# First-norm squares added on VectorE before one sum on TensorE, and a wider column of ones in the own-key sum

## The chip, the core and the metric

The kernel runs on one core of a Trainium2 chip. The metric is the device time of one execution in microseconds (us). The engines are TensorE (PE; its weight loads are listed apart as PEld), VectorE (DVE), ScalarE (ACT), GpSimd (POOL) and SyncE (SP, which issues the DMA transfers). They run their own queues in order and wait for each other by semaphores.

## The reference

One layer of a streaming encoder: 512 frames, 1024 channels, float32. What touches the change:

```python
def rmsnorm(x, g):
    y = x32 * lax.rsqrt(jnp.mean(x32 * x32, axis=-1, keepdims=True) + EPS)
    return (y * g).astype(x.dtype)
...
h = rmsnorm(x, norm_mix_g[l])
z = h @ w_in[l]      # all projections of three branches
...
# branch B, in chunks: decayed attention of each frame over the keys up to itself, and a carried state
attn = jnp.einsum("bhtk,bhsk,bhtsk->bhts", qx, kx, decay)
```

The three branches are a softmax attention with forget gates (6 heads), a gated linear recurrence (4 heads of 128 keys, 96 values) and a convolution module (256 channels, 31 taps). They are projected, merged by sigmoid gates, projected again and added to x; a second RMS norm and a gated feed-forward block of width 2816 follow.

## The kernel before

**Layout.** x lies transposed: eight tiles x0 to x7 of 128 channels by 512 frames. Each float32 product is made of three TensorE matmuls: both operands are split into a high part (suffix h; wh for weights), a rounded copy made by ScalarE, and a low part (l; wl), the remainder made by VectorE. A weight unit (`wunit`, L320) is thus a DMA to wr, a ScalarE cast to wh and a VectorE subtraction to wl; there are three buffers of each.

**The first norm.** The products start from x times the norm's gain; the factor of each frame, 1/rms, is multiplied in later, when a product leaves PSUM. The factor needs the sum of the squares of 1024 channels, which lie on partitions of eight tiles. ScalarE squares each tile into n1sq0 to n1sq7. `norm_rstd` (L425) then multiplies every 128 frames of every square tile (as the weights) with 32 columns of 1/1024 and adds all eight tiles up in PSUM: 4 x 8 matmuls into n1ms. Twelve small VectorE instructions (nv, nrt, nry, nra) take the inverse root: `rt1`, one factor for each frame, frames on partitions. `spread` (L411) transposes it on TensorE (n1rT), copies the row (n1row) and sends it through DRAM to all partitions: `rb1`, the tile n1rB. The second norm (L965) works the same way, but hands over one tile, which GpSimd has added up, so that it has 4 matmuls (n2ms).

**Who needs the factors.** The first product, him (values of branch B), has frames on partitions: four PSUM banks, evacuated by ScalarE with `rt1` to hv. The products behind it, cb, ca, cb, ca, hf, hq, f0m and so on, have frames along the free axis and are evacuated by VectorE with n1rB. Products may hold five of the eight PSUM banks.

**Own-key sum.** In each of the four heads of branch B (`hgrn_head`, L546) the product of the first frame of each 128 with its own key is summed over the 128 key channels: a matmul with one column of ones as weights gives one row (pa), which ScalarE copies to the attention tile (at).

**Order.** Nothing is issued as the code stands. Every call is recorded (`record`, L101) and a planner (`schedule`, L138) plays the kernel through with its own cost for each instruction (`cost`, L235), and writes the order of every engine's queue from that: an instruction is placed where its inputs are due and its engine is free, the lowest priority number first. Priorities are the order of the code plus a base: FIRST (first loads and splits), WPREP (weight units), STAT (squares, sums and factor of the first norm), EVAC (evacuations), then everything else, such as the him matmuls and the 31-tap convolution (cv). The planner's cost of a TensorE instruction goes by the wider of the output and the weights. So a changed instruction can change the order of the queues everywhere behind it. A line number of the trace is mostly L109, the call that issues; instructions are told apart by their tiles.

Of the kernel before, what the change touches and what calls it, by code (L numbers as in the profile page):

```python
# [15 lines left out]
ALU = mybir.AluOpType  # L16
# [13 lines left out]
NM = S // P  # L30
# [246 lines left out]
def body(ctx: ExitStack, tc, xT, wct, wt3, wt1, wdn, par, cst, rst, msk, out):  # L277
# [8 lines left out]
    nc = Plan(tc.nc, CAPS)  # L286
# [6 lines left out]
    def slot(name, dt=F32, kind=None):  # L293
        return nc.tile(spool, [P, S], dt, "s", nm(name), ("s", kind) if kind else ("s",))

    def tiny(name, n, dt=F32):
        return nc.tile(tpool, [P, 32], dt, "tiny", nm(name), ("tiny",))[:, :n]
# [4 lines left out]
    def bank(name, kind="aux"):  # L302
        return nc.tile(ppool, [P, S], F32, "ps", nm(name), ("ps", kind))
# [5 lines left out]
    def pc(name, i=0, n=1):  # L309
        o, _ = PCOLS[name]  # L310
        return pr[:, o + i:o + i + n]

    def cc(name):
        o, w = CCOLS[name]
        return cs[:, o:o + w]

    ident, ones, big = cc("ident"), cc("ones"), cc("big")
# [51 lines left out]
    def split_scaled(src, g, name):  # L369
        hi = slot(name + "h", F32R)  # L370
        nc.scalar.activation(hi, src, AF.Copy, scale=g)
        lo = slot(name + "l", F32R)
        nc.vector.scalar_tensor_tensor(lo, src, g, hi.bitcast(F32), op0=ALU.mult, op1=ALU.subtract)
        return hi, lo
# [73 lines left out]
    xg, w0, sums = [], [], []  # L448
# [3 lines left out]
    def first_weights():  # L452
        k0, k1 = cuts[len(w0)]
        src = wt3[k0 // 2][:, (k0 % 2) * 384:(k0 % 2) * 384 + (k1 - k0) * 384]
        w0.append(wunit(src, (k1 - k0) * 384, f"hi{len(w0)}", FIRST))

    for kt in range(KT):
        with nc.at(FIRST):
            if kt == 0:
                nc.sync.dma_start(pr, par)  # L460
            nc.sync.dma_start(xs[kt], xT[:, kt, :])
        if kt in (0, 1, 3):
            first_weights()
        with nc.at(FIRST):
            xg.append(split_scaled(xs[kt], pc("g1", kt), f"x{kt}"))
        with nc.at(STAT):
            q = slot(f"n1sq{kt}")
            added = nc.scalar.activation(q, xs[kt], AF.Square)
            sums.append(q)
    first_weights()  # L470
    with nc.at(FIRST):
        nc.sync.dma_start(cs, cst)
# [73 lines left out]
    def hgrn_head(h, xf, xq):  # L546
# [50 lines left out]
        for li, L in enumerate(LEVELS):  # L597
# [16 lines left out]
            else:  # L614
# [3 lines left out]
                                        op=ALU.add)  # L618
# [24 lines left out]
        pr0 = tiny("pr0", NM)  # L643
# [1 line left out]
        nc.vector.tensor_tensor(pr0, pr0,  # L645
                                xq.rearrange("p (c t) -> p c t", t=P)[:, :, 0], op=ALU.mult)
        pa = bank("pa")
        nc.tensor.matmul(pa[:1, :NM], ones[:, :1], pr0, start=True, stop=True)
        nc.scalar.copy(atc[:1, :, 0], pa[:1, :NM])
        pi = bank("pi")  # L650
        last = []
# [228 lines left out]


    hgrn_head(0, *hgrn_gemm(0))
    fox_qk(0)
    hgrn_head(1, *hgrn_gemm(1))
    fox_qk(1)
    fox_v()
    hgrn_head(2, *hgrn_gemm(2))
    hgrn_head(3, *hgrn_gemm(3))
    hgrn_norm()
# [64 lines left out]
    for n in range(KT):  # L954
        ps = gemm_c(47 + n, merged, f"wo{n}")
        with nc.at(EVAC):
            nc.vector.tensor_tensor(x1[n], ps, x1[n], op=ALU.add)
            xg2.append(split_scaled(x1[n], pc("g2", n), f"x2{n}"))
            q = slot(f"n2sq{n}")
# [117 lines left out]
```

## Time and profile before

| | |
|---|---|
| median of 3 runs | 826.54 us (826.02 to 826.95) |
| the profiled execution, its time | 826.6 us |
| its span, first to last instruction | 824.8 us |
| TensorE busy | 818.1 us, 99% |
| VectorE busy | 491.0 us, 60% |
| ScalarE busy | 334.4 us, 41% |
| GpSimd busy | 70.3 us, 9% |
| mean granted TensorE clock | 0.996 |

Busy time is summed over the instructions of an engine; the ends of matmuls, which are pipelined, are modelled, so starts are the better guide to TensorE's pace. The granted clock is a share of full speed.

### The profile page before, as it was taken

What the parts mean: (1) busy time and instruction counts of PE and PEld (TensorE: products, weight loads), DVE (VectorE), ACT (ScalarE), POOL (GpSimd) and SP (SyncE); (2) the same over time, 40 slices, a digit from 0 to 9 for tenths busy, and PEclk for the clock granted to TensorE, in tenths of its full rate; (3) what the DMA queues carried; (4) which work ended last, traced back from release to release, by engine and by line L of the source; (5) the groups of instructions that cost most, each with busy time, mean ns of one, the idle gap of its engine ahead of it and who ended that gap; (6) DMA issues with size and microseconds to landing.
All of it is one profiled execution on the core that took longest, in us unless ns stands there. A gap on an engine that the chain in (4) does not pass through costs nothing.

```text
span 824.8 us, 10354 instructions
## 1 busy us (share of the span) xinstructions
PE 818.1 (99%) x4055; PEld 693.2 (84%) x4055; DVE 491.0 (60%) x794; ACT 334.4 (41%) x545; POOL 70.3 (9%) x56
## 2 busy tenths in 40 slices
PE   8999999999999999999999999999999999999998
PEld 7989899878988888888888888888888888888888
DVE  5278898888867787744755465555555555323221
ACT  7234755655636426633334343333333333222110
POOL 1000000000000000111533111111111111000000
PEclk9899999999999999999999999999999999999999
DMA  7322122232112122233432232223322233333320
GB/s 261 124 90 90 58 85 77 88 100 96 52 40 103 65 90 102 94 111 114 153 115 84 95 116 103 83 97 103 103 99 82 101 102 96 103 109 116 108 84 26
DMA packets 26238, 80.75 MB, mean 98 GB/s; under 512 B 2982, under 2 KB 3782, under 8 KB 26188
## 3 DMA queue, kind: packets, MB, share of 16 engines
q1 hardware_dynamic: 26188, 80.08, 29.0%
q8 instruction: 32, 0.52, 0.3%
q14 instruction: 18, 0.15, 0.1%
HBM read 77.94 MB, written 2.13 MB: 97 GB/s over the span
## 4 chain that ended last, share of the span: by engine, by line
PE 98%; DMA 1%; SPq 0%; ACT 0%; issue 0%; DVE 0%
PE gl L109 16%; PE dn L109 15%; PE ug L109 15%; PE uv L109 15%; PE wo L109 5%; PE br L109 5%; PE hq L109 3%; PE hf L109 3%; PE pl L109 3%; PE fvm L109 2%; PE f0m L109 2%; PE f1m L109 2%; PE hg L109 2%; PE sp L109 2%; PE him L109 2%; PE cb L109 1%
## 5 line engine op out<-in xcount | busy, mean ns | idle before, releaser
L109 DVE TENSOR_TENSOR wl_wd<-wr_wd,wh_wd 128x1024 fp32r<-128x1024 f32 (+1 forms) x24 | 27.3, 1136 | 65.9 <-ACT wh_wd L109 65.9
L109 ACT CAST wh_wd<-wr_wd 128x1024 fp32r<-128x1024 f32 (+1 forms) x24 | 23.6, 983 | 85.6 <-PE dn L109 81.8
L109 DVE TENSOR_TENSOR wl_ug<-wr_ug,wh_ug 128x1024 fp32r<-128x1024 f32 x22 | 27.0, 1225 | 49.7 <-ACT wh_ug L109 49.7
L109 POOL TENSOR_TENSOR gr<-gr,gr 128x512 f32<-128x512 f32 x16 | 25.0, 1565 | 368.1 <-DVE gr L109 364.4
L109 POOL TENSOR_TENSOR fy<-fy,n2rB 128x512 f32<-128x512 f32 x22 | 28.9, 1317 | 207.8 <-ACT fy L109 207.8
L109 ACT CAST wh_gl<-wr_gl 128x1024 fp32r<-128x1024 f32 x24 | 25.3, 1053 | 48.5 <-PE gl L109 22.8
L109 DVE SCALAR_TENSOR_TENSOR cv<-xca,pr,cv 128x511 f32<-128x511 f32 (+29 forms) x60 | 43.5, 730 | 0.4
L109 ACT CAST wh_uv<-wr_uv 128x1024 fp32r<-128x1024 f32 x22 | 23.2, 1053 | 44.4 <-PE ug L109 37.0
L109 ACT CAST wh_ug<-wr_ug 128x1024 fp32r<-128x1024 f32 x22 | 23.2, 1054 | 30.8 <-PE uv L109 23.3
L109 DVE SCALAR_TENSOR_TENSOR fy<-ug,pr,fy 128x511 f32<-128x511 f32 (+1 forms) x44 | 32.8, 748 | 1.0 <-ACT fy L109 0.3
L109 DVE TENSOR_TENSOR gr<-gl,n1rB 128x512 f32<-128x512 f32 x24 | 16.6, 691 | 27.1 <-PE gl L109 27.1
L109 DVE TENSOR_TENSOR wl_gl<-wr_gl,wh_gl 128x1024 fp32r<-128x1024 f32 x24 | 31.5, 1311 | 1.2 <-ACT wh_gl L109 1.1
L109 DVE TENSOR_TENSOR wl_uv<-wr_uv,wh_uv 128x1024 fp32r<-128x1024 f32 x22 | 27.0, 1225 | 8.5 <-ACT wh_uv L109 8.5
L109 DVE TENSOR_TENSOR ug<-ug,n2rB 128x512 f32<-128x512 f32 x22 | 15.1, 691 | 25.4 <-PE ug L109 25.3
L109 ACT ACTIVATE fy<-fy 128x512 f32<-128x512 f32 x22 | 13.9, 632 | 39.7 <-DVE fy L109 39.6
L109 PEld LDWEIGHTS pl<-ql,kl 128*128 128x128 f32 (+2 forms) x224 | 20.8, 161 | 1.8 <-issue 0.4
L109 DVE TENSOR_TENSOR x<-dn,x 128x512 f32<-128x512 f32 (+1 forms) x9 | 5.7, 632 | 27.8 <-PE dn L109 27.8
L109 PE MATMUL pl<-ql,kl 128*128 128x64 f32 (+2 forms) x224 | 20.8, 243 | 0.0
L109 DVE TENSOR_TENSOR gr<-gr,br 128x512 f32<-128x512 f32 x24 | 16.2, 682 | 6.7 <-PE br L109 6.7
L109 ACT ACTIVATE fy<-ug,pr 128x512 f32<-128x512 f32 x22 | 17.8, 811 | 1.9 <-DVE ug L109 1.9
L109 DVE TENSOR_TENSOR d<-bm 128x520 f32<-128x520 f32 (+5 forms) x24 | 18.1, 774 | 0.0
L109 PE MATMUL sp<-qk,qk 128*128 128x128 f32 (+7 forms) x48 | 18.0, 394 | 0.0
(1128 smaller groups left out, 2574.6 us busy)
## 6 DMA issues: line engine op xcount, KB each, us to landing
wr_gl<-wct SPq DMA_DIRECT2D x24, 512.0 KB, 3.2
wr_ug<-wct SPq DMA_DIRECT2D x22, 512.0 KB, 3.2
wr_uv<-wct SPq DMA_DIRECT2D x22, 512.0 KB, 3.2
wr_wd<-wdn SPq DMA_DIRECT2D x16, 512.0 KB, 3.5
x<-xT SPq DMA_DIRECT2D x16, 256.0 KB, 3.7
wr_wb<-wct SPq DMA_DIRECT2D x8, 512.0 KB, 3.2
wr_wo<-wct SPq DMA_DIRECT2D x8, 512.0 KB, 3.1
wr_wd<-wdn SPq DMA_DIRECT2D x8, 384.0 KB, 3.1
```

What stands on the lines that cost most here:

```text
L109: op.fn = lambda: fn(*args, **kw)
```

## The change

The squares of the second to eighth tile are added on VectorE to the first, in place, so that `norm_rstd` gets one tile in place of eight. In the own-key sum the weights are all 128 columns of ones in place of the first, and the result fills all 128 partitions of the bank; the copy behind it still reads the first.

```diff
@@ -466,7 +466,10 @@
         with nc.at(STAT):
             q = slot(f"n1sq{kt}")
             added = nc.scalar.activation(q, xs[kt], AF.Square)
-            sums.append(q)
+            if kt:
+                nc.vector.tensor_tensor(sums[0], sums[0], q, op=ALU.add)
+            else:
+                sums.append(q)
     first_weights()
     with nc.at(FIRST):
         nc.sync.dma_start(cs, cst)
@@ -645,7 +648,7 @@
         nc.vector.tensor_tensor(pr0, pr0,
                                 xq.rearrange("p (c t) -> p c t", t=P)[:, :, 0], op=ALU.mult)
         pa = bank("pa")
-        nc.tensor.matmul(pa[:1, :NM], ones[:, :1], pr0, start=True, stop=True)
+        nc.tensor.matmul(pa[:, :NM], ones, pr0, start=True, stop=True)
         nc.scalar.copy(atc[:1, :, 0], pa[:1, :NM])
         pi = bank("pi")
         last = []
```

## Rows read from the trace of the kernel before

**Rows 1.** The page, busy us (share of the span) and instructions by engine.

```profile
PE 818.1 (99%) x4055; PEld 693.2 (84%) x4055; DVE 491.0 (60%) x794; ACT 334.4 (41%) x545; POOL 70.3 (9%) x56
```

**Rows 2.** The page, the chain that ended last, by engine.

```profile
PE 98%; DMA 1%; SPq 0%; ACT 0%; issue 0%; DVE 0%
```

**Rows 3.** Waits of TensorE: us in total, times, longest us.

```profile
PE him L109 <- ACT wh_hi L109: 2.4, 2, 1.5
```

**Rows 4.** The chain in order of time: start us, us, what.

```profile
15.53 0.36 PE n1ms L109 x4
15.89 1.12 PE him L109 x6
...
21.56 0.43 PE him L109 x2
21.99 6.75 PE n1ms L109 x50
28.74 6.19 PE him L109 x24
...
40.55 5.44 PE ca L109 x24
```

**Rows 5.** Windows: busy us by engine; then granted clock, DMA share, GB/s.

```profile
10.00:12.00 2.00, 0.53 (x3) 0.21 (x2) 1.68 (x3) 1.77 (x3) 0.00 (x0) 1.00 1.06 408
...
15.40:24.20 8.80, 8.80 (x66) 8.80 (x64) 4.37 (x4) 6.55 (x12) 0.00 (x0) 1.00 0.69 224
26.00:32.60 6.60, 6.60 (x27) 6.60 (x27) 1.97 (x12) 0.00 (x0) 1.22 (x2) 0.50 0.18 65
```

**Rows 6.** Timeline of TensorE around an n1ms pair: start us, us, engine, operation.

```profile
15.99 0.33 PE L109 MATMUL him<-wh_hi,x3h 128*128 128x384 f32 x1
...
16.68 0.33 PE L109 MATMUL him<-wh_hi,x4l 128*128 128x384 f32 x1
...
17.25 0.33 PE L109 MATMUL him<-wh_hi,x4l 128*128 128x384 f32 x1
```

**Rows 7.** Timeline of TensorE around the second norm's sum.

```profile
464.81 0.39 PE L109 MATMUL ug<-x26l,wh_ug 128*128 128x512 f32 x1
465.04 0.97 PE L109 MATMUL n2ms<-cs,n2sq 128*128 128x32 f32 x8
...
466.17 0.39 PE L109 MATMUL ug<-x27h,wh_ug 128*128 128x512 f32 x1
```

**Rows 8.** Timeline of VectorE, 44 to 47 us.

```profile
44.10 0.69 DVE L109 TENSOR_TENSOR xcb<-cb,n1rB 128x512 f32<-128x512 f32 x1 [1.39 <-DMA n1rB<-n1dr]
...
46.82 0.69 DVE L109 TENSOR_TENSOR xca<-xca,xcb 128x512 f32<-128x512 f32 x1
```

**Rows 9.** Timeline of ScalarE, the last four squares.

```profile
18.37 2.19 ACT L109 ACTIVATE n1sq<-x 128x512 f32<-128x512 f32 x4
```

**Rows 10.** Timeline of VectorE, 14 to 31 us.

```profile
18.50 1.23 DVE L109 TENSOR_TENSOR wl_cb<-wr_cb,wh_cb 128x1024 fp32r<-128x1024 f32 x1 [0.51 <-ACT wh_cb L109]
...
28.78 0.16 DVE L109 TENSOR_SCALAR nv<-n1ms 128x4 f32<-128x4 f32 x1 [4.63 <-PE n1ms L109]
...
30.96 0.16 DVE L109 SCALAR_TENSOR_TENSOR nry<-nra,nry 128x4 f32<-128x4 f32 x1
```

**Rows 11.** Timeline of TensorE and its weight loads, first own-key sum.

```profile
75.23 0.34 PE L109 MATMUL f0m<-wl_f0u,x2h 128*128 128x384 f32 x1
75.50 0.09 PEld L109 LDWEIGHTS pa<-pr,cs 128*1 128x1 f32 x2 [0.25 <-issue]
...
75.91 0.34 PE L109 MATMUL f0m<-wh_f0u,x3l 128*128 128x384 f32 x1
```

**Rows 12.** Windows, the stretch of the heads and the convolution.

```profile
44.00:312.00 268.00, 268.00 (x1532) 232.11 (x1531) 222.92 (x446) 137.00 (x292) 0.00 (x0) 1.00 0.24 80
```

**Rows 13.** Timeline of ScalarE and TensorE, first head's keys.

```profile
79.23 0.70 ACT L109 ACTIVATE kh<-bm 128x128 f32<-128x128 f32 x2 [1.37 <-DVE bm L109]
...
80.79 0.27 PE L109 MATMUL khT<-cs,kh 128*128 128x128 f32 x1
```

## The prediction

> **What bounds the kernel now.** I read the busy line of the page first: TensorE is busy for 818.1 of 824.8 us, VectorE for 491.0, ScalarE for 334.4 [rows 1]. Next the chain that ended last: 98% of it is TensorE [rows 2]. Then the waits with TensorE as the one that waits: apart from the warm-up's, there are two, 2.4 us together, and both end at ScalarE's cast of a first weight, before 12 us [rows 3]. So from then on nothing holds TensorE up, and what its queue contains sets the end. A piece of work taken out of that queue is worth its whole length; one added on another engine costs nothing until TensorE has to wait for it.
>
> The chain in order of time shows the place of the change [rows 4]. The sums of the first norm (n1ms) come as 64 passes, because each of the 32 matmuls in the source is run as two. The first fourteen are put between the matmuls of the first product (him) as the squares come in, and fifty stand in one block of 6.75 us. Behind that block, 24 him matmuls take 6.19 us. The windows say why so long: the granted clock is 0.50, the level of 1.2 GHz, from 26.00 to 32.60 us, after TensorE had done nothing but n1ms passes for about four us; earlier, from 15.40 to 24.20, it is 1.00, that is 2.4 GHz [rows 5].
>
> **The change, part by part.** *Taken out of TensorE's queue.* At full clock him matmuls follow each other every 0.1725 us (four steps between 15.99 and 16.68) [rows 6]. From the first n1ms pass at 15.53 to the end of the block at 28.74 there are 13.21 us, and in them 28 him matmuls (six pieces of the chain, the first and the last are shown), which alone need 28 x 0.1725 = 4.83 us [rows 4]. So the 64 passes cost 13.21 - 4.83 = 8.38 us. The 24 him matmuls behind the block need 24 x 0.1725 = 4.14 us at full clock and took 6.19: the low clock cost 2.05 us more [rows 4, 5, 6]. I take that back in full, since the engine's queue holds only him matmuls and a short burst in its place; the bound on the other side is that none comes back. Together 10.43 us.
>
> *Put in.* Four matmuls, eight passes, remain. The second norm already does exactly this: its eight n2ms passes stand between two ug matmuls that start 1.36 us apart with one more such step in between [rows 7]; at 5.44 / 24 = 0.227 us a step [rows 4], 1.36 - 0.45 = 0.91 us. Net gain on the path: 9.52 us.
>
> *Seven adds on VectorE.* No add of two whole tiles out of SBUF stands in this stretch; the nearest is the product xca of the same shape, 0.69 us [rows 8]; seven make 4.8 us. VectorE is busy for 4.37 of the 8.80 us from 15.40 on [rows 5], which leaves 4.4, so they fill the free time there and run on a little behind it. The last square ends at 20.56 [rows 9]. The last add ends 0.69 us later at the earliest, 21.25. At the latest, four adds wait until the weight part wl_cb is done at 19.73 and one has pushed that back by 0.69; with 0.04 between dependent instructions (twelve from nv to nry start 0.198 us apart and last 0.16) the end is 19.73 + 0.69 + 4 x 0.73 = 23.3 [rows 10]. TensorE's work hides this: without the early passes it reaches the 24 him matmuls at 21.99 - 1.63 = 20.36 (1.63 is what the first fourteen cost, 8.38 - 6.75) and is done with them at 24.50 [rows 4, 6]. An add can also stand in front of a low weight part of him on VectorE and make it 0.69 us late; TensorE has other him matmuls meanwhile, so the price is between 0 and about 0.7 us. I take 0.4.
>
> *What is late next.* n1ms then ends near 25.4, not at 28.7. The twelve small instructions behind it take 2.34 us [rows 10], so the factors for him are there near 28. In the old run the row factors were in use 13.0 us behind that chain (31.12 to 44.10) [rows 8, 10], so now near 41. TensorE starts cb at 25.4 (old: 34.9) and needs a bank of him again one product, 5.44 us, later, at 30.9: ScalarE has some 3 us to empty the first. The five banks for products would be full at 25.4 + 5 x 5.44 = 52.6, long after 41. No wait is due, though the margin between TensorE and the row factors is 9.5 - 3 = 6.5 us smaller than it was.
>
> *The own-key sum.* A pass pair of pa sits between two f0m matmuls that start 0.68 us apart: 0.68 - 2 x 0.1725 = 0.335 us [rows 6, 11]. Its weight load starts after 0.25 us in which the load side did nothing [rows 11]; I saw that in three of the four heads. With 128 columns it becomes the form of n1ms: a pair of those costs 17.25 - 16.68 - 0.345 = 0.225 us [rows 6], one of n2ms 0.91 / 4 = 0.23. Gain 0.11 us for each of four heads, 0.44 in all; the bound on the other side is that the idle 0.25 us stays in front of a pair of 0.225, 0.14 us more than now, a loss of 0.56 in all. I take the gain, since no pass of n1ms or n2ms shows such a gap. The Trainium skill (TensorE: Matmul & The Clock Gate, section LDWEIGHTS) speaks against this edit: a weight load's time goes by its columns, 1.2 per ns. By that rule the eight loads become 0.106 us longer each, 0.85 us, and the total gain would be 8.3 us in place of 9.6. The trace has the two narrow loads of a pair in 0.09 us, but with the idle time in front of them.
>
> *Sum.* 9.52 + 0.44 - 0.4 = 9.56 us. The profiled execution took 826.6 us beside its span of 824.8, and the median of the runs is 826.54, so both start from one number: 826.6 - 9.6 = 817.0 us. What a measurement here can tell from no change is 0.2%, 1.7 us.
>
> **Rivals.** *The new sums hold TensorE (partly given back).* The queue is written in a fixed order; if the eight passes stand in front of the last 24 him matmuls, everything behind waits for the last add: from 20.36 to 23.3 at most, 2.9 us. If the clock falls there too and those 24 run as slowly as before, 2.05 more are lost. The gain is 9.56 - 4.95 = 4.6, the time 822.0. For it: the passes have a better priority than him. Against: a pass is queued only where its input is due, and between 10 and 12 us, with TensorE busy for 0.53 of 2 us, the clock stayed at 1.00 [rows 5]. The Trainium skill (TensorE: Matmul & The Clock Gate, section HAM oscillation) says that waits between bursts of matmuls throttle the array again, which would make this case likelier; here the one fall that the trace shows came without a wait.
>
> *VectorE takes over.* From 44 to 312 us it is busy for 222.92 of 268 us, 83%, with the clock at 1.00 [rows 12]. If everything in it kept its date relative to the row factors, which move by 3 us only, TensorE would get back 6.5 of its 9.5 us by waiting: 826.6 - 3.1 = 823.5. If TensorE's head start of 6.5 us also has to be paid again in the heads, the sign turns: TensorE takes up the transposed keys (khT) at 80.79, when the first two tiles were ready at 79.93, a margin of only 0.86 us [rows 13]. A new order that makes each of the four heads late by more than 9.56 / 4 = 2.4 us decides for slower; late by 4 us each, the time is 826.6 - 9.6 + 16 = 833. Against it: 45 us of VectorE in that stretch are idle, much of the rest is the long convolution that can give way, and the heads hang on TensorE's own products, which come earlier by the full gain.
>
> *The clock falls elsewhere, or n1ms was hidden.* The second can't be: no wait stands behind it. For the first, 6.6 us at half clock are worth 3.3 us of work [rows 5], so a like fall elsewhere leaves 820.3.
>
> **How the numbers follow.** Full gain (815.2 to 819): 0.64. Partly given back, by the held queue, a fall of the clock or VectorE (819 to 824.9): 0.18, most of it below 822. No change (within 1.7 us): 0.04. Slower, the heads: 0.06. More than the sum, because the rewritten order also suits the stretch behind: 0.08. The range of 815.2 to 822.0 takes in the first and most of the second; its lower end is the bound without any allowance (826.6 - 9.96 = 816.6) less 1.4 us for a luckier order, a choice. Faster 0.90, same 0.04, slower 0.06.
>
> **What would show it.** Right: eight n1ms passes of about 0.9 us near 21 to 25 us; the granted clock 1.00 in every window from 5 to 45; cb starts near 25.4; pa without idle time in front of its load and about 0.225 us a pair; seven adds of 0.69 us behind squares, none waited for by TensorE; every later product 9 to 10 us earlier, up to the end. Wrong: TensorE waiting for n1sq, or for a weight part wl_hi; a clock of 0.50 somewhere between 20 and 40; a row of waits of TensorE on khT, kl or the row factors between 60 and 230, by which the lead shrinks from stage to stage.

## The result and the profile after

The changed kernel takes 816.8 us (816.55 to 817.3, 4 runs) against 826.68 us before, a ratio of 0.988 with a 95% interval of 0.9865 to 0.9899. The forecast was 817.0.

The chain of the changed kernel in order of time (start us, us, what) answers to [rows 4]:

```profile
10.83 13.89 PE him L109 x80
24.71 1.39 PE cb L109 x6
26.11 0.81 PE n1ms L109 x8
26.92 4.17 PE cb L109 x18
31.09 0.11 PE n1rT L109
31.20 5.49 PE ca L109 x24
```

All him matmuls now follow each other without a break, the eight passes stand inside cb, and ca starts at 31.20 in place of 40.55: a lead of 9.35 us.

The two profiled executions do not begin alike, and the difference is not the change's. Until about 10.5 us the him matmuls here start every 0.32 us, in the execution before every 0.17 us (the granted clock reads 1.00 in both, so that row does not tell the two apart); the earlier kernel then waits for the cast of the third weight unit of him. The first matmul with that unit, in the changed kernel and in the kernel before (timeline):

```profile
12.07 0.33 PE L109 MATMUL him<-wh_hi,x2h 128*128 128x384 f32 x1
```

```profile
11.79 0.45 PE L109 MATMUL him<-wh_hi,x2h 128*128 128x384 f32 x1 [1.48 <-ACT wh_hi L109]
```

So the changed kernel sets out 0.2 to 0.3 us later (0.28 by these starts; the matmul behind a wait takes 0.1 us more), and the change's own lead at ca is 9.5 to 9.6 us, beside the 9.52 us of the sum before its allowance of 0.4 for the adds. In the kernels below this date lies between 11.46 and 12.58. The first matmul of the last product, dn, starts at 691.12 in place of 700.96, so the lead is 9.84 us there. No stage behind gave anything back.

The windows of the changed kernel (busy us of PE, PEld, DVE, ACT, POOL, then the granted clock, DMA share, GB/s) answer to [rows 5, 12]:

```profile
15.40:24.20 8.80, 8.80 (x52) 8.80 (x51) 8.13 (x11) 6.22 (x11) 0.00 (x0) 1.00 0.68 221
24.20:32.60 8.40, 8.40 (x43) 7.07 (x43) 4.17 (x14) 2.75 (x4) 1.90 (x2) 1.00 0.54 188
...
44.00:312.00 268.00, 268.00 (x1534) 233.35 (x1533) 223.77 (x456) 138.40 (x297) 0.00 (x0) 1.00 0.24 81
```

The clock is 1.00 where it was 0.50. VectorE went from 4.37 to 8.13 us of work in the first window, and TensorE is busy throughout all three. Its waits (us in total, times, longest), all of them, answer to [rows 3]:

```profile
PE warm L109 <- DVE warm L109: 1.2, 1, 1.2
PE him L109 <- ACT wh_hi L109: 0.7, 1, 0.7
```

On VectorE, the last adds and the instructions behind them (timeline), to be read beside [rows 10]:

```profile
19.63 1.49 DVE L109 TENSOR_TENSOR n1sq<-n1sq,n1sq 128x512 f32<-128x512 f32 x2
21.51 1.22 DVE L109 TENSOR_TENSOR wl_ca<-wr_ca,wh_ca 128x1024 fp32r<-128x1024 f32 x1 [0.39 <-ACT wh_ca L109]
22.65 1.41 DVE L109 TENSOR_TENSOR n1sq<-n1sq,n1sq 128x512 f32<-128x512 f32 x2
...
26.96 0.16 DVE L109 TENSOR_SCALAR nv<-n1ms 128x4 f32<-128x4 f32 x1
...
29.50 0.16 DVE L109 SCALAR_TENSOR_TENSOR nry<-nra,nry 128x4 f32<-128x4 f32 x1
31.98 1.23 DVE L109 TENSOR_TENSOR wl_ca<-wr_ca,wh_ca 128x1024 fp32r<-128x1024 f32 x1 [2.32 <-ACT wh_ca L109]
```

The last add ends at 24.06, 1.9 us before TensorE reaches the passes at 25.94. What turned out to matter is the order below that: the twelve small instructions end at 29.66, and only then comes the second wl_ca.

### The profile page after: what moved, and what is told of

It is laid out like the page before. It is cut to its first block, busy times and chain, and to the rows that moved or that the text cites. A ratio compares the mean times of both kernels' runs of the same rounds, so it can differ in the third digit from the quotient of the medians.

```text
span 815.0 us, 10258 instructions
## 1 busy us (share of the span) xinstructions
PE 809.9 (99%) x3999; PEld 686.7 (84%) x3999; DVE 495.4 (61%) x801; ACT 334.3 (41%) x545; POOL 71.0 (9%) x56
## 4 chain that ended last, share of the span: by engine, by line
PE 99%; DMA 0%; ACT 0%; DVE 0%; SPq 0%; issue 0%; ACTq 0%
PE gl L109 17%; PE dn L109 15%; PE ug L109 15%; PE uv L109 15%; PE wo L109 5%; PE br L109 5%; PE hf L109 3%; PE hq L109 3%; PE pl L109 3%; PE him L109 2%; PE fvm L109 2%; PE f0m L109 2%; PE f1m L109 2%; PE hg L109 2%; PE sp L109 2%; PE cb L109 1%
```

## The experiments

The ratios are to the kernel before, run on the same chip; its medians there were 826.7 to 827.0 us.

**Each part alone.** First the adds without the wide ones:

```diff
-        nc.tensor.matmul(pa[:, :NM], ones, pr0, start=True, stop=True)
+        nc.tensor.matmul(pa[:1, :NM], ones[:, :1], pr0, start=True, stop=True)
```

> The adds on VectorE alone, the own-key sum with one column as before. If TensorE's queue alone sets the time: 9.1 to 9.5 us of the gain stay, 817.2 us, the clock 1.00 throughout, and a pass pair of the own-key sum is back at 0.335 us. If the width of the weights were the price (the rule that a weight load goes by its columns): 0.85 us less than the changed kernel, 816.0. If the gain came from a luckier order of the queues, this other order could give anything from 815 to 822, with waits of TensorE that come and go.

Measured: 817.1 us, ratio 0.989 (0.9876 to 0.9904). The adds make nearly the whole gain, and in a partly different order of the queues.

The wide ones without the adds are the second hunk of the change on the kernel before.

> The 128 columns of ones alone, 32 sums on TensorE as before. Queue theory: 0.44 us less than before, 826.1, the block of 50 passes and the low clock still there. Rule of the weight load's columns: 0.85 us more, 827.4. Order theory: a change of over 1 us either way, since the order behind is rewritten.

Measured: 826.3 us, ratio 0.9994 (0.9984 to 1.0003). The forecast gain of 0.44 us lies within this interval, and so does nothing at all; the loss of 0.85 us (1.001) does not.

To see the pairs themselves, the changed kernel with one column in the same order of the queues:

```diff
-        nc.tensor.matmul(pa[:, :NM], ones, pr0, start=True, stop=True)
+        op = nc.tensor.matmul(pa[:1, :NM], ones[:, :1], pr0, start=True, stop=True)
+        op.dur = 0.003 + P * 1.667e-3
```

> The changed kernel with one column of ones again, but the planner is given the cost of the wide matmul, so that all queues keep the changed kernel's order. Queue theory: 0.44 us slower than the changed kernel, 817.2, and every product behind the fourth own-key sum 0.4 us later in the trace. Weight load rule: 0.85 us faster, 816.0. Order theory: what differs between this and the adds alone is order only.

Measured: 817.3 us, ratio 0.9888 (0.9875 to 0.9901), not to be told from the changed kernel by time. The timeline tells them apart. The second head's sum in the changed kernel:

```profile
112.07 0.34 PE L109 MATMUL f1m<-wh_f1u,x7h 128*128 128x384 f32 x1
112.25 0.28 PE L109 MATMUL pa<-pr,cs 128*128 128x4 f32 x2
...
112.64 0.34 PE L109 MATMUL f1m<-wl_f1u,x7h 128*128 128x384 f32 x1
```

and with one column, the weight load of the pair first:

```profile
112.90 0.09 PEld L109 LDWEIGHTS pa<-pr,cs 128*1 128x1 f32 x2 [0.25 <-issue]
...
112.64 0.34 PE L109 MATMUL f1m<-wh_f1u,x7h 128*128 128x384 f32 x1
112.91 0.19 PE L109 MATMUL pa<-pr,cs 128*1 128x4 f32 x2
...
113.31 0.34 PE L109 MATMUL f1m<-wl_f1u,x7h 128*128 128x384 f32 x1
```

Between the f1m matmuls on both sides lie 112.64 - 112.07 = 0.57 us with 128 columns and 113.31 - 112.64 = 0.67 with one. The load is shorter but comes 0.25 us late. The difference is 0.10 us, as was priced (0.11). Over all four sums it shows less: the first cb starts 0.51 us later in this execution (25.06 against 24.55), dn 0.77 us later (691.89 against 691.12), so 0.26 us lie between.

**The own-key matmul, 44 times.** Since 0.4 us is below what a measurement tells, the same small matmul goes in front of each product of the up-projection, which then overwrites the bank; once with one column and once with 128:

```diff
         ps = bank(name, "mm")
+        if name[:2] in ("ug", "uv"):
+            with nc.after(nc.ops[-1]):
+                op = nc.tensor.matmul(ps[:1, :NM], ones[:, :1], pc("g2", 0, NM), start=True, stop=True)
+            op.dur = 0.003 + P * 1.667e-3
         gemm_unit(ps, w, acts, True, True)
```

> The changed kernel with one more matmul in front of each of the 44 products of the up-projection: one column of ones by four columns, into the bank that the product then overwrites; the result stays the same. The planner is given the wide matmul's cost. Queue theory with the gap in front of a one-column load: 44 x 0.335 = 14.7 us, 831.5, and idle time of 0.25 us before each of these loads. Weight load rule: the load itself is all but free, the pair costs 0.1 us or less, 821.

> As the run before in the same order of all queues, but with all 128 columns of ones. Queue theory: 44 x 0.225 = 9.9 us, 826.7, no idle time before the loads, 4.8 us less than with one column. Weight load rule: 0.21 us more for each than with one column, 9.3 us slower than that run.

Measured: 832.2 us, ratio 1.0068 (1.0049 to 1.0087), with one column; 828.9 us, 1.0023 (1.0013 to 1.0033), with 128 (`ps[:, :NM], ones`). The first meets its expectation, the second is 2.2 us over it. The weight loads in front of the uv products (count, busy us, mean ns, idle us before them and what ended it), with one column and with 128:

```profile
L109 PEld LDWEIGHTS uv<-pr,cs 128*1 128x1 f32 x44 | 1.9, 80 | 7.8 <-PE ug L109 6.3 <-issue 1.4
```

```profile
L109 PEld LDWEIGHTS uv<-pr,cs 128*128 128x128 f32 x44 | 8.3, 188 | 1.7
```

That is 0.35 us of idle time for each of 22 pairs with one column and under 0.1 us with 128. The first matmul of all ug products, by tile (duration ns min/median/max, first and last start), with one column, with 128, and in the changed kernel:

```profile
L109 PE MATMUL ug<-x20h,wh_ug x22: 497/497/504, 451.2 to 695.3; 128*128 128x512 f32 x22
```

```profile
L109 PE MATMUL ug<-x20h,wh_ug x22: 475/475/476, 450.4 to 691.1; 128*128 128x512 f32 x22
```

```profile
L109 PE MATMUL ug<-x20h,wh_ug x22: 388/389/389, 450.7 to 680.2; 128*128 128x512 f32 x22
```

First and last lie 42 products apart: 5.812, 5.731 and 5.464 us each. So one pair costs 0.35 us with one column and 0.27 with 128. The narrow one is dearer, by 0.08 us; the price of the wide one in the sum (0.225) was 0.04 too low for this place.

**The 64 passes without the low clock.** The kernel before, its last 48 passes spread:

```diff
+    him = [o for o in nc.ops if o.eng == "tensor"][-24:]
+    i0 = len(nc.ops)
     with nc.at(STAT):
         rt1, rb1 = norm_rstd(sums, "n1")
+    n1 = [o for o in nc.ops[i0:] if o.eng == "tensor"][:32]
+    for g in range(6):
+        for o in n1[8 + 4 * g:12 + 4 * g]:
+            o.deps.add(him[4 * g + 3])
```

> The kernel before, with all 64 passes, but the last 48 in six groups of eight, each behind four of the last 24 him matmuls. If the low clock came from TensorE doing nothing but these passes for several us, it stays at 1.00 now; the passes then cost 1.63 + 0.2 + 6 x 0.91 = 7.3 us in place of 8.38 and the him matmuls get their 2.05 us back: 3.1 us faster than before, 823.5. If the passes lower the clock however they stand, it is 0.50 again from about 26 us for as long, and the time is 825.5 to 826.6.

Measured: 823.4 us, ratio 0.9956 (0.9941 to 0.9971). That is 3.6 us less than the kernel before on its chip (2.4 to 4.9). Windows and chain of this run:

```profile
20.00:32.00 12.00, 12.00 (x89) 11.91 (x89) 1.73 (x3) 2.74 (x5) 1.22 (x2) 1.00 0.55 187
```

```profile
21.93 0.78 PE him L109 x4
22.71 0.81 PE n1ms L109 x8
...
```

The same instructions, in another order, with the clock at 1.00. The first cb starts at 31.29 in place of 34.77; of these 3.5 us, 0.2 lie at the start, and 3.3 stand beside the 3.1 that were worked out. So about a third of the change's gain is the clock, and nearly all the rest is the passes taken out.

**The held queue.** The rival that the prediction priced, brought about:

```diff
+    for o in him + [o for o in nc.ops[i0:] if o.eng == "tensor"][5:]:
+        o.deps.add(n1[3])
     with nc.after(*first_sig):
```

(him as above; n1 the four n1ms matmuls; the list behind it the matmuls of cb and ca, both units of each.)

> The changed kernel, but the last 24 him matmuls and the first cb and ca are made to wait for the eight n1ms passes, so that these stand in front. This is the rival that the prediction priced. TensorE has nothing to do from 20.2 us until the last add, which ended at 24.1 in the changed kernel and may end a little earlier now: 3 to 4 us of waiting. With the clock at 1.00 behind the wait: 820 to 821. If it falls to 0.50 behind the wait as the rule on waits says, 2 us or more on top: 822 to 823. If TensorE's early work was hidden behind something else: no change, 816.8.

Measured: 824.0 us, ratio 0.9965 (0.9952 to 0.9978): 7 us of the gain gone, more than was expected. TensorE's wait, its clock (windows), and the him matmuls behind it (chain):

```profile
24.04 1.08 PE L109 MATMUL n1ms<-cs,n1sq 128*128 128x32 f32 x8 [3.65 <-DVE n1sq L109]
```

```profile
24.00:25.00 1.00, 0.96 (x9) 0.96 (x9) 0.00 (x0) 0.00 (x0) 0.00 (x0) 1.00 1.05 348
25.00:26.00 1.00, 1.00 (x6) 1.00 (x6) 0.71 (x5) 0.00 (x0) 0.00 (x0) 0.69 0.99 307
26.00:27.00 1.00, 1.00 (x5) 1.00 (x5) 0.86 (x5) 0.00 (x0) 0.36 (x1) 0.50 0.92 367
...
172.00:180.00 8.00, 8.00 (x29) 6.41 (x29) 3.16 (x9) 1.83 (x5) 0.00 (x0) 0.79 0.11 44
```

```profile
25.12 5.81 PE him L109 x24
```

The wait is 3.65 us, and the 24 him matmuls take 5.81 us, 1.7 more than 4.14. Together 5.3, the lag of ca (36.53 against 31.20). Another 1.9 us come with a second fall of the clock after 172 us; br lags by 7.2 us (337.6 against 330.4).

**How much later may the sum come?** Fourteen adds in place of seven:

```diff
             if kt:
+                half = slot(f"half{kt}")
+                nc.vector.tensor_tensor(half, sums[0], q, op=ALU.add)
                 nc.vector.tensor_tensor(sums[0], sums[0], q, op=ALU.add)
```

> Each of the seven adds is made twice on VectorE (the first goes to a spare tile), 4.8 us more of VectorE's time and a chain that ends some 4 us later. Queue theory: hidden, since the evacuation of him has about 4 us and the row factors more than that: 816.8 to 817.5. If VectorE's time in the first 45 us, or the later row factors, counted: up to 4.8 us more, 821.6.

Measured: 827.0 us, ratio 1.0002 (0.9994 to 1.0011). The whole gain is gone, and my expectation with it. TensorE's largest waits:

```profile
PE n1ms L109 <- DVE n1sq L109: 3.5, 1, 3.5
PE him L109 <- ACT wh_hi L109: 3.4, 2, 2.3
PE n1rT L109 <- DVE nry L109: 2.4, 1, 2.4
```

The waits of him are those of the start. With a clock of 0.50 behind the other two, ca takes 7.21 us in place of 5.49. Was it VectorE's time, or the place of the sum in the queues? Three more kernels ask. One add more only (the two added lines under `if kt == KT - 1`):

> The changed kernel with one add more on VectorE, in front of the last: the sum comes some 0.7 us later. In the changed kernel the last add ends 1.9 us before TensorE reaches the passes. If that margin is what decides, the add is hidden: 816.6 to 817.5. If each add costs what fourteen did on average (10 us for seven more): 1.4 us more, 818.3.

Measured: 821.9 us (819.5 to 822.7), ratio 0.9927 (0.9913 to 0.9941). An instruction of 0.69 us costs 5 us in the median. TensorE does not wait for the sum; the timelines of VectorE and of ScalarE show where the time goes:

```profile
29.87 0.16 DVE L109 SCALAR_TENSOR_TENSOR nra<-nry 128x4 f32<-128x4 f32 x1
31.93 1.23 DVE L109 TENSOR_TENSOR wl_ca<-wr_ca,wh_ca 128x1024 fp32r<-128x1024 f32 x1 [1.90 <-ACT wh_ca L109]
33.07 0.16 DVE L109 TENSOR_TENSOR nra<-nra,nv 128x4 f32<-128x4 f32 x1
33.27 0.16 DVE L109 SCALAR_TENSOR_TENSOR nry<-nra,nry 128x4 f32<-128x4 f32 x1
```

```profile
30.86 1.04 ACT L109 CAST wh_ca<-wr_ca 128x1024 fp32r<-128x1024 f32 x1 [5.32 <-PE cb L109]
```

and that of TensorE:

```profile
30.66 0.39 PE L109 MATMUL cb<-x7h,wl_cb 128*128 128x512 f32 x1
33.48 0.27 PE L109 MATMUL n1rT<-cs,nry 128*4 128x128 f32 x1 [2.44 <-DVE nry L109]
33.51 0.48 PE L109 MATMUL ca<-x0h,wh_ca 128*128 128x512 f32 x1
```

The planner has written the second wl_ca, with its better priority, between the tenth and the eleventh of the twelve small instructions. Its cast on ScalarE, though, starts only when TensorE is done with cb (30.86). So the last two small instructions wait for wl_ca, the transpose n1rT waits for them, and ca, whose own inputs are ready, stands behind n1rT. TensorE is idle for 2.44 us, ca takes 7.09 us in place of 5.49 with the clock at 0.51 from 34 to 36 us, and the clock falls once more near 171 us: br is 6.0 us behind the changed kernel in this profile. In the changed kernel the twelve were all in front of wl_ca.

This profile is of an execution of 822.7 us. The six executions differ by their mean granted clock: 819.5 us at 1.000, 820.1 and 821.5 at 0.998, 822.3 to 822.7 at 0.996. So without a fall of the clock the one add cost 2.7 us, about the wait itself; the rest of the 5 us comes with falls that not every execution has.

That it is the order, and not the added 0.7 us, is read from the traces: the twelve start 0.8 us later here than in the changed kernel (27.78 against 26.96), where they had been done 1.3 us before n1rT's turn (29.66 against 30.93). No run adds the time and keeps the order.

If the order is the cause, another order should bring the fourteen adds' loss back. Six banks for products let ca go ahead (`"mm": 5` to `"mm": 6`), once with fourteen adds and once, as the control, with seven:

> The fourteen adds again, but the planner may give products six PSUM banks in place of five, so that it writes ca in front of the eight n1ms passes. If the earlier run with fourteen adds lost its 10 us because the passes and the row's transpose stood in TensorE's queue before their inputs were there: most of it comes back, 817 to 820, the wait of TensorE for the sums is under 1 us and the clock stays at 1.00. If VectorE's 4.8 us themselves were the cost: 825 or more, as before.

> The control: the changed kernel, seven adds, with six banks for products. TensorE had no wait to lose, so 816.5 to 818; a luckier order would show as less than 816.

Measured: 823.4 us, ratio 0.9959 (0.9947 to 0.9971), and 817.5 us, 0.989 (0.9873 to 0.9907). Only a third of the loss came back, so the expectation failed in its size, and the clock did not stay at 1.00. The wait for the sum is gone, but TensorE waits 3.5 us for n1rT: now it is the next unit, wl_hf, that stands among the twelve. The chain shown here is from an execution of 826.4 us at a mean clock of 0.991; the ten go down to 822.0 us at 0.998.

```profile
37.53 1.23 DVE wl_hf L109
...
40.15 0.37 PE n1rT L109
40.52 7.93 PE cb L109 x24
```

Last, the adds on GpSimd (`nc.gpsimd` for `nc.vector` in the new line):

> The seven adds on GpSimd, as the second norm does it, 1.6 to 1.8 us each: the last ends near 26.5 us, and the passes stand at about 26.3 us in TensorE's queue. Queue theory: a wait of 0 to 1.5 us, 817 to 818.5. If GpSimd's adds also hold VectorE's weight parts up: TensorE waits for wl_hi or wl_cb and the time is over 819.

Measured: 825.9 us, ratio 0.9986 (0.9975 to 0.9997). The timelines of GpSimd and of VectorE:

```profile
15.54 10.04 POOL L109 TENSOR_TENSOR n1sq<-n1sq,n1sq 128x512 f32<-128x512 f32 x5 [15.09 <-ACT n1sq L109]
```

```profile
16.21 3.74 DVE L109 TENSOR_TENSOR wl_hi<-wr_hi,wh_hi 128x768 fp32r<-128x768 f32 x2 [0.20 <-ACT wh_hi L109]
19.88 2.32 DVE L109 TENSOR_TENSOR wl_cb<-wr_cb,wh_cb 128x1024 fp32r<-128x1024 f32 x1
```

Each slows the other: the first five adds take 2.0 us each, and VectorE's weight parts 1.87 and 2.32 us in place of 0.95 and 1.22. The time is far over the 817 to 818.5 expected, but TensorE does not wait for a weight part, as the other case had it: it waits 2.4 us for the sum and 2.2 us for the transpose.

## Why the prediction was right, and where it was not

**The queue of TensorE sets the end.** Held: the lead of 9.35 us at ca is 9.84 at dn, and only the early waits are left. The heads and VectorE gave nothing back.

**Passes and clock.** Held: the first cb starts 10.22 us earlier (24.55 against 34.77), 10.4 to 10.5 apart from the start; the sum had 10.43. The two parts are shown apart: with the 64 passes kept and the clock at 1.00 the kernel takes 823.4 us, forecast 823.5; the 6 to 7 us from there to the changed kernel are the passes taken out and the own-key sums. The eight passes stand at 25.94 inside cb, not near 21 to 25 in front of it, and cost what those of the second norm do: cb matmuls at 25.71 and 27.07 lie 1.36 us apart with one more step between them.

**Seven adds.** They cost nothing on the path, and the 0.4 us allowed for a late weight part of him was not needed: from 12.07 to the first cb at 24.55 the 72 him matmuls start every 0.173 us. That 817.0 lies so near 816.8 is in part luck, since this 0.4 stands against the 0.2 to 0.3 us by which the changed kernel's execution set out later. The last add ended at 24.06, later than the bound of 23.3: the first wl_ca came in between, which the working had left out.

**What is late next: the step that failed, though not the number.** I worked out that the factors of him and the row factors had 3 us and 11 us of room. That counted banks and finishing times, and left out that in-order queues hold what stands behind a waiting instruction. No wait came, as forecast, but not for the reason given. The timelines of TensorE and of ScalarE in the changed kernel:

```profile
30.93 0.27 PE L109 MATMUL n1rT<-cs,nry 128*4 128x128 f32 x1
30.96 0.47 PE L109 MATMUL ca<-x0h,wh_ca 128*128 128x512 f32 x1
```

```profile
31.86 1.99 ACT L109 ACTIVATE hv<-him,nry 128x384 f32<-128x384 f32 x4
```

ca did not need a bank of him: it started (30.96) before ScalarE began to empty the first (31.86). It does need n1rT out of its way, n1rT needs the twelve small instructions, and these lie among VectorE's weight units, which wait for TensorE's own progress. On the chip n1rT had 1.3 us of room; in the planner's order one more add of 0.69 us was enough to put a weight unit among the twelve, at a cost of 5 us in the median. That the changed kernel stands on the good side of this is luck: its planner happened to write that order. The range of 815.2 to 822.0 had not been drawn for that reason.

**The own-key sum.** The mechanism held: no gap in front of the wide load, 0.10 us less for a pair on the trace, 0.08 in the product stream. The forecast 0.44 us for the four cannot be told in the time alone; the lead grows from 9.35 at ca to 9.84 at dn, and two other pairs of traces put the four sums at 0.26 us (one column in the same order) and 0.35 (the wide ones alone, cb 0.35 and dn 0.70 us earlier than before). The Trainium skill (TensorE: Matmul & The Clock Gate, section LDWEIGHTS) is borne out for the load itself: 80 ns with one column, 188 with 128, a difference of 108 ns beside its 106. Carried over to the kernel's time, as the prediction did for the rival case, it gave the wrong sign, since the short load began 0.25 us late. Why it does stays open.

**The rivals.** The held queue is real when brought about, and dearer than priced (7 us, not 4.95): the wait was 3.65 us in place of 2.9, the him matmuls behind it lost 1.7 in place of 2.05, and a second fall of the clock took 1.9 more. The Trainium skill (same page, section HAM oscillation) said that the clock falls behind a wait; the waits of 3.65 and 2.44 us here were each followed by 0.50 in the profile. It is not so every time: the wait of 2.3 us at the start with fourteen adds was followed by 1.00, and one execution with one more add has a mean clock of 1.000.

## What to carry to other kernels

When one engine's queue sets the end, price a change by what it takes out of that queue, at the duration and at the clock that the trace shows there; several us of nothing but tiny matmuls cost their own time and, here, half the clock of the good matmuls behind them. Then follow each operand of the next instructions in that queue back through the other in-order queues, and ask what stands among its producers and what that waits for: a small late step behind a big prefetch that waits for the busy engine is a cycle, and 0.7 us of added work cost 5 us here. A work item that is free on an idle engine is free only as long as it doesn't change that order.

## What the runs showed of the hardware

- A load of one column of weights (80 ns) started 0.25 to 0.35 us late between wide matmuls, where 128 columns (188 ns) did not; a transpose of four columns (n1rT) had no such gap in the profiles before and after the change.
- The clock fell to 0.50 behind waits of TensorE (3.65 us in the held queue, 2.44 us with one more add) and, with TensorE busy all the time, inside the block of n1ms passes at 26.00 us. A second fall came between 170 and 175 us in the five profiled kernels that had lost time early, behind the score matmuls sp; in the changed kernel the same matmuls ran with the clock at 1.00. The executions of one kernel differ in such falls: the adds alone took 818.9 us at a mean clock of 0.998 in one of five executions and 817.0 to 817.3 at 1.000 in the others. What sets them off stays open.
- GpSimd's adds took 2.0 us beside VectorE's subtractions of two SBUF tiles, in place of 1.78 in the second norm, and those subtractions about 1.9 times as long as alone. The Trainium skill (GPSIMD Engine Reference, section Specifications) says that the two engines share their SBUF interfaces; these numbers agree.
